# A hybrid decoder step on one core: where weight-block operations, gate stores and small stores stand in their queues

## The chip, the core and the metric

The kernel runs on one core of a Trainium2 chip. A core has five engines that each work through an instruction queue of their own, in order: TensorE (PE in the profile, its weight loads apart as PEld), VectorE (DVE), ScalarE (ACT), GpSimd (POOL) and SyncE (SP). Matrix products go from SBUF to PSUM by PE; DVE and ACT read PSUM and SBUF; GpSimd reads and writes SBUF alone. Transfers between the device's memory (DRAM below) and SBUF are issued as instructions of SP, ACT or POOL and carried out by 16 DMA engines that all three share. An instruction that waits for a semaphore holds everything behind it in its queue, a DMA issue as well as a computation.

The metric is the device time of one execution in microseconds. A time below is that of single executions, or the median over several.

## The reference

One decoder layer over a prompt of 2048 tokens and 8 single-token samples, all in f32, width 1024. Cut to what matters here:

```
hn  = rmsnorm(x) * (1 + scale) + shift              # shift, scale, gate from silu(c) @ w_ada + b_ada
xa, za, q, k, v, glr, zg = split(hn @ w_in)
xc  = conv4(xa); gx, ga = sigmoid(block-diagonal products of xc)
a   = exp(8 * ga * log_sigmoid(lambda))
h_t = a_t * h_(t-1) + sqrt(1 - a_t**2) * gx * xc    # the scan of the recurrence
y_lru = h * silu(za)
o, S = gated linear attention(q, k, v, log_sigmoid(glr @ w2 + b2) / 16)    # 4 heads, dk 128, dv 256
y_gla = rmsnorm(o) * silu(zg)
x   = x + gate * (concat(y_lru, y_gla) @ w_out);  y = rmsnorm(x)
```

## The kernel before

Every large product is made three times, as high*high, high*low and low*high parts in a fast number format, so each weight exists as a high and a low part. The prompt is worked in two halves of 1024 tokens. The main order is: for half 0, the four attention heads in the order 3, 0, 1, 2, each followed by one to three of the eight recurrence tiles; then a middle stage in which the gates `zg` and two recurrence tiles of half 1 are made by products over seven block combinations instead of eight (`seven`, `product`, L1511); then the four heads and five tiles of half 1; last the output projection (`Pair.product`, L1797), also with seven blocks. The ordinary projection is `project` (L650 to L652: 24 matmuls over 8 blocks of the width), the values are made by `value_mm` (L335 to L337: also 24).

The seven-block products need combinations of weight blocks. They are prepared on the side, during half 0 and half 1, by two chains of small steps:

- `pair_weights(n)`, n = 0 to 4, one pair of `w_in` column blocks each: two loads of 512 KB into the tile `tr` issued by POOL (L749), four DVE subtractions (L753) in two phases, then two phases in which ACT rounds (L758), DVE subtracts (L759) and POOL stores the parts to `twd` (L761). The tile has one buffer: the loads of pair n+1 wait until the stores of pair n have been read out. After the last phase the next pair's loads are issued.
- `out_weights`, steps s = 0 to 15, of `w_out`: two loads of 256 KB into `r` by POOL (L806), two DVE products with the gate `g` (L827), then four DVE subtractions (L827), for every second group of four steps two splits (ACT L831, DVE L832), and 7 to 9 stores to `wd` and `wd2` by POOL (L841, L834). Then the next step's loads are issued (`again`); at s = 0 and 8, and where the chain is taken up again, `begin` also loads the gate and waits longer.

Both run on a clock of their own, counted in units. `tick(u)` stands in the main program after each projection (1 unit for a projection of 264 to 512 columns, with exceptions of half a unit for each block of values and for `product`, and n/512 in `gates_ahead`), and `after(u, f)` puts f into a heap to be traced at the first tick that brings the clock to the present value plus u. So a delay in units is a delay in the order of the program, not in time. The phases inside a step follow at 0.5 units. `behind(V)` puts a step's DVE instructions directly behind the last DVE instruction traced before: whatever DVE instruction comes later in the program waits behind them.

`lru_last_a` sets `outw["stop"]` after the first of the last three recurrence tiles of half 0; the chain then ends with the step in hand, and `close_sp` takes it up again at the next step when half 1 begins.

The gates of half 0 are made in `gate_silu`; for the second part of the half it also makes the gate of the 8 samples, a tile of 128x8 (`zq`), and stores it (L1117). `xa_load` splits a recurrence tile's own small weights and stores the parts, 256 KB (L1331). `gates_seven` makes the gates of half 1 for three heads in the middle stage and stores each 128x512 tile to `zgd` from ACT (L1572); `gates_ahead` does so for the first head (L1599), each store right after its `silu2`. `silu` is an ACT instruction (L1092) and a DVE instruction (L1093); a store waits for the second.

## Time and profile before

| what | value |
|---|---|
| time, median of 3 executions | 1502.39 us (1500.59, 1502.39, 1505.2) |
| the profiled execution's own time | 1495.52 us |
| its span, from the first to the last instruction | 1493.7 us |
| mean granted TensorE clock in it | 0.989 of full |
| DMA, mean over the span | 204 GB/s; 9.6% of the DMA engines' time for what POOL issued, 46.4% SP, 4.3% ACT |

The profile is one execution. Its page gives each engine's busy time, then the same in 40 slices, the DMA queues, the chain of work that ended last, and the costliest groups of instructions. Further views list the waits (who waited for whom, how long in all, how often, the longest), all instructions in order of time (start, duration, engine, line, operation, tiles, shapes; in square brackets the idle time of the engine before it and what ended that), one line's instructions with their waits, and busy time, granted clock and DMA share in windows of time. "PE tp L1006 <- DVE xb L991" reads: PE, about to write the tile `tp` in line 1006, waited for DVE's write of `xb` in line 991. Idle time of an engine counts for the result only where PE, the busiest one, ends up waiting for it.

### The profile page before, as it was taken

To read this page: it belongs to the slowest core of one execution; us is meant where nothing else is said; L and a number is where in the kernel's file an instruction comes from. 1 tells how busy PE (TensorE), PEld (TensorE's weight loads), DVE (VectorE), ACT (ScalarE), POOL (GpSimd) and SP (SyncE) were. 2 spreads that over 40 slices of the span, in tenths; PEclk is the share of its full clock that TensorE was granted. 3 is DMA by queue.
4 is the path that set the end of the run, shared out by engine and by line. 5 is a ranking of instruction groups with operands and counts; after the bars stand their busy time and mean duration, and the time that the engine had idled before them with its cause. 6 is when DMAs were issued, how large, how long until landed. Compare 5 with 4: busy or idle time off the path is not lost.

```text
span 1493.7 us, 23572 instructions
## 1 busy us (share of the span) xinstructions
PE 1437.0 (96%) x8741; PEld 1259.8 (84%) x8741; DVE 1052.3 (70%) x2473; ACT 690.7 (46%) x1255; POOL 175.1 (12%) x288
## 2 busy tenths in 40 slices
PE   8999898999998999899999989999999999999998
PEld 6888877798887888777799989999998887778886
DVE  5757555766766678774539857576679887588886
ACT  4654443454355257634435453544556732244342
POOL 1200211222223121200011310000000000000000
PEclk9999999999999999999999999999999999999999
DMA  9656875667567466376865744635353757793452
GB/s 331 248 180 212 269 255 168 198 211 246 181 214 247 150 217 218 142 254 206 280 218 173 237 152 146 191 131 178 131 173 110 279 184 274 266 349 123 148 174 113
DMA packets 172120, 305.33 MB, mean 204 GB/s; under 512 B 13858, under 2 KB 103618, under 8 KB 169565
## 3 DMA queue, kind: packets, MB, share of 16 engines
q1 hardware_dynamic: 121333, 235.35, 46.4%
q0 software_dynamic: 16032, 48.28, 9.6%
q10 hardware_dynamic: 34640, 20.19, 4.3%
q8 instruction: 69, 1.13, 0.3%
q14 instruction: 46, 0.38, 0.1%
HBM read 188.51 MB, written 115.33 MB: 203 GB/s over the span
## 4 chain that ended last, share of the span: by engine, by line
PE 53%; DVE 5%; ACT 4%; DMA 3%; issue 2%; POOL 1%; ACTq 0%; POOLq 0%; DVEq 0%
PE acc L1797 12%; PE tp L1797 8%; PE acc L1511 6%; PE acc L650 5%; PE acc L652 5%; PE acc L651 5%; PE acc L335 1%; PE acc L337 1%; PE acc L336 1%; DMA w<-parts 1%; PE po L1040 1%; PE tp L1006 1%; DVE cv L1234 1%; ACT L945 1%; DMA wd<-r 1%
## 5 line engine op out<-in xcount | busy, mean ns | idle before, releaser
L650 PE MATMUL acc<-hh,w 128*128 128x512 f32 (+3 forms) x1112 | 388.5, 350 | 3.3 <-POOL hh L201 1.5
L651 PE MATMUL acc<-hl,w 128*128 128x512 f32 (+3 forms) x1112 | 377.0, 339 | 0.0
L652 PE MATMUL acc<-hh,w 128*128 128x512 f32 (+3 forms) x1112 | 376.7, 339 | 0.2 <-DVE w L300 0.2
L650 PEld LDWEIGHTS acc<-hh,w 128*128 128x128 f32 x1112 | 211.2, 190 | 23.2 <-POOL hh L201 2.4
L651 PEld LDWEIGHTS acc<-hl,w 128*128 128x128 f32 x1112 | 211.4, 190 | 16.5 <-DVE hl L202 0.2
L652 PEld LDWEIGHTS acc<-hh,w 128*128 128x128 f32 x1112 | 210.8, 190 | 17.0 <-DVE w L300 0.6
L1797 PE MATMUL acc<-w,a 128*128 128x512 f32 (+1 forms) x792 | 184.8, 386 | 0.0
L1797 PEld LDWEIGHTS acc<-w,a 128*128 128x128 f32 x792 | 146.8, 188 | 33.2 <-issue 3.4
L335 PE MATMUL acc<-w,hh 128*128 128x256 f32 (+1 forms) x508 | 146.4, 288 | 7.1 <-DVE vl L924 4.0
L337 PE MATMUL acc<-w,hl 128*128 128x256 f32 (+1 forms) x508 | 144.1, 284 | 0.2 <-DVE hl L225 0.2
L336 PE MATMUL acc<-w,hh 128*128 128x256 f32 (+1 forms) x508 | 143.8, 283 | 0.0
L1797 PE MATMUL tp<-w,a 128*128 128x512 f32 x564 | 136.0, 391 | 0.0
L1797 PEld LDWEIGHTS tp<-w,a 128*128 128x128 f32 x564 | 105.2, 188 | 26.8 <-issue 5.2
L335 PEld LDWEIGHTS acc<-w,hh 128*128 128x128 f32 x508 | 96.8, 191 | 10.1 <-DVE vl L924 4.6
L337 PEld LDWEIGHTS acc<-w,hl 128*128 128x128 f32 x508 | 97.1, 191 | 0.4 <-DVE hl L225 0.4
L336 PEld LDWEIGHTS acc<-w,hh 128*128 128x128 f32 x508 | 96.7, 190 | 0.1
L1234 DVE SCALAR_TENSOR_TENSOR cv<-xa,vecT,cv 128x512 f32<-128x512 f32 (+2 forms) x120 | 76.8, 644 | 9.1 <-ACT cv L1232 8.7
L1092 ACT ACTIVATE zs<-acc 128x512 f32<-128x512 f32 (+3 forms) x71 | 34.6, 489 | 102.6 <-PE acc L652 93.4
L1647 ACT CAST a<-s 128x512 fp32r<-128x512 f32 x61 | 36.5, 620 | 95.5 <-issue 36.2
L1093 DVE SCALAR_TENSOR_TENSOR zs<-zs,acc 128x512 f32<-128x512 f32 (+3 forms) x71 | 39.0, 549 | 45.5 <-ACT zs L1092 45.4
L923 ACT CAST vh<-acc 128x256 fp32r<-128x256 f32 x56 | 20.7, 371 | 78.9 <-PE acc L337 66.3
L924 DVE TENSOR_TENSOR vl<-acc,vh 128x256 fp32r<-128x256 f32 x56 | 23.4, 421 | 44.9 <-ACT vh L923 44.6
(389 smaller groups left out, 2713.3 us busy)
## 6 DMA issues: line engine op xcount, KB each, us to landing
parts<-w SPq DMA_DIRECT2D x37, 1024.0 KB
w<-parts SPq DMA_DIRECT2D x28, 1024.0 KB
wr<-in_w_in_dram SPq DMA_DIRECT2D x44, 512.0 KB
a<-mixd SPq DMA_DIRECT2D x63, 256.0 KB
w<-wd SPq DMA_DIRECT2D x12, 1024.0 KB
w<-twd SPq DMA_DIRECT2D x20, 512.0 KB
mixd<-zs ACTq DMA_DIRECT2D x34, 256.0 KB
wada<-in_w_ada_dram SPq DMA_DIRECT2D x16, 512.0 KB
```

What stands on the lines that cost most here:

```text
L335: PE.matmul(ps, hh[:, kt, c], hi[:, kt % 4], start=kt == 0, stop=False)
L336: PE.matmul(ps, hh[:, kt, c], lo[:, kt % 4], start=False, stop=False)
L337: PE.matmul(ps, hl[:, kt, c], hi[:, kt % 4], start=False, stop=kt == KT - 1)
L650: PE.matmul(ps[:, :n], hi[:, kt], a, start=kt == 0, stop=False)
L651: PE.matmul(ps[:, :n], hi[:, kt], b, start=False, stop=False)
L652: PE.matmul(ps[:, :n], lo[:, kt], a, start=False, stop=kt == KT - 1)
L1092: S.activation(z, ps, AF.Tanh, scale=0.5)
L1093: V.scalar_tensor_tensor(z, z, 1.0, ps, op0=OP.add, op1=OP.mult)
L1234: V.scalar_tensor_tensor(cv[:, cq], xa[:, cq.start + k:cq.stop + k], cw[k], cv[:, cq], op0=OP.mult, op1=OP.add)
L1511: PE.matmul(ps, w[:, u, k], x[v][k], start=start and (k, u, v) == (0, 0, 0), stop=(k, u) == (3, 1), skip_group_check=True)
L1647: S.copy(t[:, 0, k], (low(t) if src is None else src)[:, k])
L1797: PE.matmul(ps, t[:, u, k], w[:, v, k, c], start=(q < 3 or ps is own) and (k, u, v) == (0, 0, 0), stop=(k, u) == (3, 1), skip_group_check= ...
```

## The change

Six places, each a line:

```
 def pair_weights(n=0):
-        after(2, lambda: one([[sub(b11, b12, b11), ...
+        after(3, lambda: one([[sub(b11, b12, b11), ...
 def again(s, g):                                        # in out_weights
             r = load(s)
-            after(2, lambda: step(s, r, g))
+            after(3, lambda: step(s, r, g))
 def gate_silu(w, s, ct):
-                SP.dma_start(zgd[ct][:, TH:], q)
+                G.dma_start(zgd[ct][:, TH:], q)
 def xa_load(j, wx=True):
             parts[j] = dpool.tile([P, 2, 2, P], F32, tag=f"wg{j}", name="parts")
-            SP.dma_start(parts[j], wg.bitcast(F32))
+            G.dma_start(parts[j], wg.bitcast(F32))
 def gates_seven(n):
             silu(z, ps)
-            S.dma_start(zgd[2 * h + dt][:, s * 512:s * 512 + 512], z)
+            G.dma_start(zgd[2 * h + dt][:, s * 512:s * 512 + 512], z)
 def gates_ahead(h):
                 z = silu2(w[dt], c0, n)
-                S.dma_start(zgd[2 * h + dt][:, c0:c0 + n], z)
+                after(0.5, lambda z=z, dt=dt, c0=c0, n=n: S.dma_start(zgd[2 * h + dt][:, c0:c0 + n], z))
                 tick(n / 512)
```

In the two chains the first operations on a loaded block are traced three units after its loads instead of two. Eight stores of sample gates, eight of small weights and twelve of gates are issued by GpSimd (`G`) instead of SyncE or ScalarE. Six stores of gates stay on ScalarE and go through the heap with a delay of half a unit. What is computed is the same.

More of the change, by code (lines that the diff above doesn't have):

```diff
@@ L773, in pair_weights @@
         halves = [split(k, x) for k, x in enumerate((b11, b22, b12, b21))]
-        after(2, lambda: one([[sub(b11, b12, b11), sub(b12, b22, b12)], [sub(b22, b22, b11), sub(b21, b21, b22)],
+        after(3, lambda: one([[sub(b11, b12, b11), sub(b12, b22, b12)], [sub(b22, b22, b11), sub(b21, b21, b22)],
                                 halves[:2], halves[2:]]))
```

## The prediction

> **What bounds the kernel now.** I read the page's busy times first, then PE's idle gaps in order of time, then what DVE did in front of each, then the granted clock around them.

> ```profile
> span 1493.7 us, 23572 instructions
> PE 1437.0 (96%) x8741; PEld 1259.8 (84%) x8741; DVE 1052.3 (70%) x2473; ACT 690.7 (46%) x1255; POOL 175.1 (12%) x288
> ```

> PE is the bound: busy for 1437.0 of 1493.7 us. The 56.7 us in which it sits idle are all that a change of order can win directly. These are its longest gaps after the start:

> ```profile
> 170.33 0.58 PE L335 MATMUL acc<-w,hh 128*128 128x256 f32 x1 [3.98 <-DVE vl L924]
> 197.46 0.38 PE L1006 MATMUL tp<-xb,e 128*128 128x128 f32 x1 [2.48 <-DVE xb L991]
> 238.63 1.94 PE L1126 MATMUL tp<-ident,on 128*128 128x128 f32 x8 [6.38 <-DVE on L1053]
> 279.59 0.59 PE L1271 MATMUL acc<-xh,wg 128*128 128x264 f32 x1 [3.51 <-DVE zs L1093]
> 480.17 0.58 PE L1006 MATMUL tp<-xb,e 128*128 128x128 f32 x1 [4.11 <-DVE xb L991]
> 875.52 0.73 PE L1006 MATMUL tp<-xb,e 128*128 128x128 f32 x3 [3.45 <-DVE xb L991]
> ```

> Each waits for DVE, for a different line each time, so the named lines aren't the cause. What is common to them stands a few microseconds earlier in DVE's queue:

> ```profile
> 168.23 0.69 DVE L753 TENSOR_TENSOR tr<-tr 128x512 f32<-128x512 f32 x1 [5.87 <-DMA tr<-in_w_in_dram]
> 195.39 1.42 DVE L753 TENSOR_TENSOR tr<-tr 128x512 f32<-128x512 f32 x2 [2.28 <-DMA tr<-in_w_in_dram]
> 231.55 0.69 DVE L753 TENSOR_TENSOR tr<-tr 128x512 f32<-128x512 f32 x1 [6.17 <-DMA tr<-in_w_in_dram]
> 278.25 0.69 DVE L753 TENSOR_TENSOR tr<-tr 128x512 f32<-128x512 f32 x1 [6.58 <-issue]
> 464.45 1.29 DVE L827 TENSOR_TENSOR r<-r,g 128x512 f32<-128x512 f32 x2 [4.84 <-DMA r<-in_w_out_dram]
> 465.78 0.41 ACT L831 CAST p<-r 128x256 fp32r<-128x256 f32 x1 [6.75 <-DVE r L827]
> 866.86 0.69 DVE L827 TENSOR_TENSOR r<-r,g 128x512 f32<-128x512 f32 x1 [4.23 <-DMA r<-in_w_out_dram]
>   DMA r<-in_w_out_dram: 17.6, 6
> ```

> DVE reaches the first operation on a weight block before the block has landed, and everything of the main path queued behind it (value evictions, normalisation, decay) waits too; at 464 ACT is held as well, by the split behind the same load. (The row at 278.25 names "issue"; its operation is the same, the first on a pair.) The last row is from the view of line 827: its 32 products waited for loads 17.6 us in 6 waits; two of them, over 3 us each, reached no PE gap of this size.

> A gap costs more than its idle time. The windows view, cut where the granted clock changes:

> ```profile
> 169.30:176.10 6.80, 5.77 (x28) 0.50 0.58 211
> 237.60:244.40 6.80, 5.77 (x25) 0.50 0.34 103
> 278.50:285.30 6.80, 5.71 (x26) 0.50 0.47 154
> 479.90:483.30 3.40, 3.13 (x13) 0.50 1.01 323
> 875.90:879.30 3.40, 3.40 (x15) 0.51 0.32 107
> ```

> Columns: window, length, PE busy (matmuls), granted clock, DMA share and GB/s. Around every gap of 3.45 us or more PE ran at half clock, 3.4 or 6.8 us long; around the one of 2.48 us it didn't. The busy time in them is 5.77 + 5.77 + 5.71 + 3.13 + 3.40 = 23.8 us; half of it, **11.9 us**, is lost. [...]

> **The change part by part: the third unit.** It removes no work. It moves the first DVE operation on a block one unit later in program order. What it must beat is the time from the last store of the block before to the landing of the new one. For a pair:

> ```profile
> 149.09 1.08 POOL L761 DMA_DIRECT2D twd<-tr  x2 [0.92 <-DVE tr L759]
> 154.27 0.92 POOL L749 DMA_DIRECT2D tr<-in_w_in_dram  x1 [4.10 <-DMA twd<-tr]
> 160.80 0.90 POOL L749 DMA_DIRECT2D tr<-in_w_in_dram  x1 [5.61 <-issue]
> DMA to landing us min/median/max: 4.5/6.4/8.7
> ```

> From the last store's issue (149.6) the two loads are issued at 154.3 and 160.8, and DVE starts on the data at 168.2: 18.6 us. How long a unit is follows from the matmul spacing:

> ```profile
> 165.97 0.28 PE L336 MATMUL acc<-w,hh 128*128 128x256 f32 x1
> 166.08 0.28 PE L337 MATMUL acc<-w,hl 128*128 128x256 f32 x1
> 286.14 0.40 PE L651 MATMUL acc<-hl,w 128*128 128x512 f32 x1
> 286.38 0.40 PE L652 MATMUL acc<-hh,w 128*128 128x512 f32 x1
> ```

> Starts are 0.11 us apart at 256 columns, 0.24 at 512. So 24 matmuls take 2.7 us for a block of values (half a unit), 2.8 for a 256- or 264-column projection and 5.6 for 512 columns (a unit each); 384 columns, between them, 4.2. Counting ticks through the loops I find which projections lie between load and first operation:

> - Pair 1 now: one of 264 columns and two blocks of values, 8.2 us; after: six blocks, 16.2. That is 8.0 more for a stall of 5.87.
> - Pair 2: three blocks and a 512 (13.7), then three of 512 (16.8): 3.1 more for 2.28.
> - Pair 3: two of 512 (11.2), then 256 + 264, 512 and 256 (14.0): 2.8 more for 6.17, short by 3.4. The chunk products of the attention head, also between them, shrink that.
> - Pair 4: 256 + 264 (5.6), then 264 + 512 + 512 (14.0): 8.4 more for 6.58.
> - `w_out` step 7, the stall at 464: four blocks (10.8), then three of 512 (16.8): 6.0 more for 4.84.
> - Step 15, the stall at 867: four blocks (10.8), then three of 384 (12.6): 1.8 more for 4.23, short by 2.4.

> What is taken from each PE gap is the smaller of gap and stall, for 480 the gap, since ACT's longer wait hung on that load too: 3.98 + 2.28 + 6.17 + 3.51 + 4.11 + 3.45 = **23.5 us**, and 11.9 of clock with it: 35.4. What stays, where the added time falls short: 3.4 + 2.4 = 5.8 at most, 0 at least with the chunk products. I take **3.0**. Both are below the gaps at which the clock fell.

> The steps also shift. The five pairs end at unit 36.5 instead of 32, and the `w_out` chain has done 8 steps instead of 12 when it is stopped, so that four more (steps 8 to 11, each six DVE operations and nine POOL transfers) run in half 1, up to unit 142.5 of 165.5, where before it was done at 123.5. They fit. What they cost there:

> ```profile
> 752.00:885.00 133.00, 126.75 (x942) 122.69 (x941) 91.92 (x302) 61.03 (x126) 30.77 (x53) 0.99 0.59 196
> 885.00:1010.00 125.00, 123.82 (x928) 118.80 (x926) 85.64 (x306) 57.77 (x126) 4.94 (x8) 1.00 0.46 148
> ```

> With four steps (752 to 885) PE idled 6.25 us, 3.45 of them the gap counted above; without steps 1.18. So four more steps cost 6.25 - 3.45 - 1.18 = **1.6 us**; the bounds are 0 and 2.8. DVE, 69% busy in both windows, has room.

> **The stores.** Sample gates and small weights leave SP's queue for POOL's, 0.55 us an issue. What they held up on SP:

> ```profile
> SPq L1117 <- DVE zq L1093: 80.1, 7, 24.7
> SPq L1331 <- DVE wg L1329: 37.8, 5, 15.4
> PE acc L652 <- DVE w L300: 0.2, 1, 0.2
> ```

> SP waited 117.9 us on these, with weight loads behind it, yet the one PE wait in half 0 for a freshly loaded weight is the 0.2 in the last row. The cover is the loads issued ahead; the gain is at most 0.2. On POOL each wait now stands in front of the block loads and stores traced after it. Those follow DVE instructions placed later still, so the wait is hidden as long as POOL keeps program order; if not, it is the slower rival below. Taken as 0.

> The twelve gates of the middle stage leave ACT for POOL, which does next to nothing there. Gain: at most PE's wait for ACT in that stage, 0.7 us; loss: a gate buffer that comes free later, bounded by the only wait of that kind (2.5 us, ACT for an earlier store). Taken as 0.

> ```profile
> PE acc L1511 <- ACT acc L1525: 0.7, 1, 0.7
>   ACT zs L1092: 2.5, 1
> 613.57 0.56 ACT L199 ACTIVATE ra<-tp,Sh,Gm 128x256 f32<-128x256 f32 x1 [4.99 <-DVE zs L1093]
> ```

> The half unit in `gates_ahead` mostly does nothing: the store goes into the heap and the very next line ticks by 0.5 or 1, which takes it out again. So ACT's 4.99 us before 613.57, spent at the first of these stores, stays. Only the fourth, due at unit 82 with the last gates of recurrence tile 7, falls behind those. That may gain or lose about a microsecond of ACT's time; 0.

> **Sum**, against the profiled execution's own 1495.5: -23.5 - 11.9 + 3.0 + 1.6 = -30.8, thus 1464.7. That execution lies 6.9 us below the median of the three shown, 1502.4; from the median it would be 1471.6. One stall more or less is worth some 6.5 us (3.5 idle, 2.9 of clock), so I hold part of that difference for stalls that also go. I take **1469 us**.

> **Rivals.**

> *The unit is too short where it counts.* Loads that land later than in this one execution, up to 8.7 us after issue where 6.4 is the median, bring back pairs 3 and 4 and step 15 in part. For: two places fall short by my count. Against: pairs 1, 4 and step 7 have 1 us or more to spare. If a third of 35.4 stays, the time is 1469 + 12 = 1481.

> *The wait only moves.* The blocks' transfers are late because the DMA engines are, and the main path's DVE work lies wherever the step falls; as many PE gaps appear elsewhere. For: DMA share 0.47 to 1.01 in the windows above. Against: of 32 products on `w_out` blocks 26 waited for no load. Time 1500, no change.

> *POOL's queue becomes the bound (slower).* In half 0 the sample stores hold POOL as they held SP, 80.1 / 7 = 11.4 us each, with the next block's loads behind them. This decides once the hold is longer than the 5.6 us of the added unit: then DVE stalls by 5.8 us again, which at 170 cost 3.98 + 2.9 = 6.9 us. Seven times that is 48: 1469 + 48 = 1517. Against it stands the order on POOL, as above, and how evenly its issues run:

> ```profile
> L761 POOL DMA_DIRECT2D twd<-tr x20: 542/542/552, 145.1 to 291.6; - x20
> ```

> [...]

> **How the numbers follow.** Forecast 0.73, unit too short 0.13, wait moves 0.05, POOL 0.09. A difference of 0.3% (4.5 us) is about what a measurement of this kernel can tell from no change. The first two are faster, the third the same, the fourth slower: 0.86, 0.05, 0.09. The forecast's own range is 1457 to 1481: from the profiled execution with nothing staying and another 3 us from the stores, to the median with 5.8 and 2.8 staying and some 5 lost at the stores. The range that also holds the second case and its worse half reaches to 1494.

> **What would show it.** Right: no DVE idle of over 2 us in front of L753 and L827; PE's idle down from 56.7 to about 38; no half clock between 20 and 1480 us; L827 from about 350 to 1000 us with its last 16 products, not 8, after 750. The store steps: L1117, L1331 and L1572 on POOL, SP's waits on the first two gone and replaced by waits for buffers, the 4.99 of ACT still there. Wrong: DVE waiting for `tr` or `r` as before (the unit), gaps of 3.4 us and more with other releasers (the wait moved), or POOL idle at L1117 and L1331 just ahead of late L749 or L806 loads.

## The result and the profile after

The changed kernel took 1477.72 us (median of 4 executions, 1475.09 to 1479.32), the kernel before, on the same chip, 1501.49 us (4 executions, 1492.67 to 1505.2). The ratio is 0.985 with a 95% interval of 0.980 to 0.989: faster by 23.8 us, where 1469 us had been forecast. The profiled execution of the changed kernel took 1479.32 us, the longest of its four, that of before was 6 us below its median; the two traces therefore differ by 16.2 us only, and the split below is of those 16.2.

From the page of the changed kernel, its first lines:

```profile
span 1477.5 us, 23587 instructions
PE 1434.1 (97%) x8741; PEld 1258.6 (85%) x8741; DVE 1050.0 (71%) x2472; ACT 690.6 (47%) x1255; POOL 188.1 (13%) x314
```

PE's idle time fell from 56.7 to 43.4 us, 13.3 less; its busy time from 1437.0 to 1434.1 us, 2.9 less. Forecast were 18.9 less idle (-23.5 + 3.0 + 1.6) and 11.9 less of half clock.

Busy time by stage, before first, then the changed kernel (columns as before: window, length, PE busy and matmuls, PEld, DVE, ACT, POOL, granted clock, DMA share, GB/s; the stages begin up to 30 us earlier in the changed kernel, the windows are the same):

```profile
100.00:300.00 200.00, 183.56 (x1168) 163.81 (x1167) 126.99 (x301) 83.11 (x158) 32.00 (x52) 0.95 0.64 209
300.00:560.00 260.00, 255.52 (x1476) 225.34 (x1475) 180.70 (x397) 124.37 (x206) 63.62 (x109) 0.99 0.64 209
560.00:760.00 200.00, 191.81 (x1018) 159.79 (x1017) 130.88 (x219) 99.48 (x152) 21.06 (x31) 1.00 0.66 225
760.00:1140.00 380.00, 367.83 (x2730) 352.82 (x2729) 266.62 (x877) 188.55 (x393) 38.48 (x66) 1.00 0.51 168
```

```profile
100.00:300.00 200.00, 197.19 (x1309) 176.20 (x1308) 138.42 (x317) 96.80 (x176) 32.42 (x54) 1.00 0.68 226
300.00:560.00 260.00, 260.00 (x1460) 227.48 (x1460) 178.62 (x397) 129.37 (x213) 52.06 (x90) 1.00 0.60 201
560.00:760.00 200.00, 190.20 (x1050) 162.97 (x1049) 117.83 (x210) 89.62 (x141) 23.27 (x36) 0.97 0.62 209
760.00:1140.00 380.00, 362.21 (x2673) 347.23 (x2672) 283.70 (x901) 190.53 (x395) 59.36 (x102) 0.99 0.53 173
```

Length less PE busy is PE's idle time. Before 560 us it falls from 16.4 + 4.5 to 2.8 + 0.0, by 18.1. From 560 to 760 it grows from 8.2 to 9.8, and from 760 to 1140 from 12.2 to 17.8. The first half pays most of what was forecast for it (18.1 of 20.1); the rest gives 7.2 us of it back.

PE's rows in order of time, at its long gaps:

```profile
177.29 0.51 PE L650 MATMUL acc<-hh,w 128*128 128x512 f32 x1 [0.91 <-DVE vl L924]
613.44 0.57 PE L1511 MATMUL acc<-hh,w 128*128 128x512 f32 x1 [3.74 <-DVE zs L1093]
724.13 0.60 PE L335 MATMUL acc<-w,hh 128*128 128x272 f32 x1 [3.38 <-DMA w<-parts]
844.49 0.41 PE L650 MATMUL acc<-hh,w 128*128 128x384 f32 x1 [2.18 <-DMA w<-parts]
941.22 0.49 PE L650 MATMUL acc<-hh,w 128*128 128x384 f32 x1 [5.05 <-DVE xb L973]
1120.39 0.44 PE L1271 MATMUL acc<-xh,wg 128*128 128x384 f32 x1 [2.64 <-ACT tx L1274]
```

All six gaps that the prediction listed are gone; the first row is what is left of the one at 170. The others are where no gap of 3 us stood before, and the half clock came with them. (The last one is not new: before, PE waited 2.4 us for the same write, at full clock.) The windows view, cut where the granted clock changes:

```profile
613.70:617.10 3.40, 3.40 (x9) 2.68 (x9) 3.40 (x4) 2.03 (x4) 0.00 (x0) 0.51 1.04 332
723.00:729.80 6.80, 5.67 (x25) 5.67 (x26) 0.71 (x4) 0.37 (x1) 2.11 (x3) 0.50 1.04 308
845.80:849.20 3.40, 3.40 (x12) 3.40 (x11) 0.47 (x1) 0.00 (x0) 1.65 (x3) 0.51 0.42 148
941.40:944.80 3.40, 3.40 (x12) 3.40 (x12) 0.56 (x2) 0.82 (x2) 1.44 (x2) 0.50 0.96 371
1122.30:1125.70 3.40, 3.40 (x17) 3.33 (x16) 3.32 (x5) 2.73 (x6) 0.00 (x0) 0.50 0.00 0
```

PE was busy for 19.3 us in these, so 9.6 us are lost to the clock where 11.9 were lost before.

DVE's waits, from the order of time and from the views of lines 753 and 827:

```profile
175.16 0.69 DVE L753 TENSOR_TENSOR tr<-tr 128x512 f32<-128x512 f32 x1 [5.00 <-DMA tr<-in_w_in_dram]
209.64 0.69 DVE L753 TENSOR_TENSOR tr<-tr 128x512 f32<-128x512 f32 x1 [4.41 <-DMA tr<-in_w_in_dram]
930.62 0.69 DVE L827 TENSOR_TENSOR r<-r,g 128x512 f32<-128x512 f32 x1 [3.37 <-DMA r<-in_w_out_dram]
...
  DMA tr<-in_w_in_dram: 9.4, 2
...
  DMA r<-in_w_out_dram: 3.4, 1
```

Two of the pairs (1 and 2) still stall DVE, by 5.0 and 4.4 us, where it was 5.87 and 2.28. PE pays nearly nothing for these. The windows view over the first two of DVE's waits, and below it over the wait of before that ended at 168.23:

```profile
170.16:175.16 5.00, 5.00 (x46) 4.94 (x42) 0.00 (x1) 0.00 (x0) 0.00 (x0) 1.00 1.06 374
205.23:209.64 4.41, 4.41 (x21) 3.60 (x21) 0.00 (x1) 0.36 (x1) 0.00 (x0) 1.00 0.82 252
```

```profile
162.36:168.23 5.87, 3.99 (x36) 3.80 (x34) 0.00 (x1) 0.00 (x0) 0.00 (x0) 1.00 1.00 271
```

Before, PE had 3.99 us of work for a wait of 5.87 and ran dry while DVE still waited; now it is busy through the whole wait. The stall of pair 1 is nearly as long as it was and stands where PE has more work ahead.

The stores are where the change puts them (a line's view: issues, ns, first and last):

```profile
L1117 POOL DMA_DIRECT2D zgd<-zq x8: 541/546/570, 111.1 to 497.9; - x8
...
L1572 POOL DMA_DIRECT2D zgd<-zq x8: 542/542/543, 667.4 to 719.2; - x8
```

### The profile page after: what moved, and what is told of

It reads as the page before. It is cut to its first block, busy times and chain, and to the rows that moved or that the text cites. A ratio compares the mean times of both kernels' runs of the same rounds, so it can differ in the third digit from the quotient of the medians.

```text
span 1477.5 us, 23587 instructions
## 1 busy us (share of the span) xinstructions
PE 1434.1 (97%) x8741; PEld 1258.6 (85%) x8741; DVE 1050.0 (71%) x2472; ACT 690.6 (47%) x1255; POOL 188.1 (13%) x314
## 4 chain that ended last, share of the span: by engine, by line
PE 65%; DVE 9%; DMA 6%; ACT 5%; issue 3%; POOL 0%; ACTq 0%; DVEq 0%; SPq 0%; POOLq 0%
PE acc L1797 12%; PE tp L1797 9%; PE acc L650 8%; PE acc L652 8%; PE acc L651 8%; PE acc L1511 6%; PE acc L335 2%; PE acc L337 2%; PE acc L336 2%; DMA w<-parts 1%; DMA mixd<-zs 1%; PE po L1040 1%; DMA xt<-in_state_gla_dram 1%; PE tp L1006 1%; PE acc L1271 1%
## 5 line engine op out<-in xcount | busy, mean ns | idle before, releaser
L651 PE MATMUL acc<-hl,w 128*128 128x512 f32 (+3 forms) x1112 | 377.4, 339 | 0.0
L652 PE MATMUL acc<-hh,w 128*128 128x512 f32 (+3 forms) x1112 | 377.0, 339 | 0.0
L651 PEld LDWEIGHTS acc<-hl,w 128*128 128x128 f32 x1112 | 210.9, 190 | 16.6 <-DVE hl L202 0.4
L652 PEld LDWEIGHTS acc<-hh,w 128*128 128x128 f32 x1112 | 210.8, 190 | 16.5
L335 PE MATMUL acc<-w,hh 128*128 128x256 f32 (+1 forms) x508 | 146.0, 287 | 5.4 <-DMA w<-parts 3.4
L337 PE MATMUL acc<-w,hl 128*128 128x256 f32 (+1 forms) x508 | 143.7, 283 | 0.0
L336 PE MATMUL acc<-w,hh 128*128 128x256 f32 (+1 forms) x508 | 143.6, 283 | 0.0
L335 PEld LDWEIGHTS acc<-w,hh 128*128 128x128 f32 x508 | 96.8, 191 | 7.9 <-DMA w<-parts 3.6
L337 PEld LDWEIGHTS acc<-w,hl 128*128 128x128 f32 x508 | 97.1, 191 | 0.0
L336 PEld LDWEIGHTS acc<-w,hh 128*128 128x128 f32 x508 | 96.7, 190 | 0.1
L1647 ACT CAST a<-s 128x512 fp32r<-128x512 f32 x61 | 36.5, 620 | 95.8 <-issue 36.8
L1092 ACT ACTIVATE zs<-acc 128x512 f32<-128x512 f32 (+3 forms) x71 | 34.6, 488 | 93.8 <-PE acc L652 84.7
L1093 DVE SCALAR_TENSOR_TENSOR zs<-zs,acc 128x512 f32<-128x512 f32 (+3 forms) x71 | 38.9, 548 | 41.7 <-ACT zs L1092 41.7
L165 ACT ACTIVATE junk<-on 128x256 bf16<-128x256 f32 x64 | 26.6, 416 | 71.7 <-DVE on L1045 70.3
```

What stands on the lines that cost most here:

```text
L335: PE.matmul(ps, hh[:, kt, c], hi[:, kt % 4], start=kt == 0, stop=False)
L336: PE.matmul(ps, hh[:, kt, c], lo[:, kt % 4], start=False, stop=False)
L337: PE.matmul(ps, hl[:, kt, c], hi[:, kt % 4], start=False, stop=kt == KT - 1)
L651: PE.matmul(ps[:, :n], hi[:, kt], b, start=False, stop=False)
L652: PE.matmul(ps[:, :n], lo[:, kt], a, start=False, stop=kt == KT - 1)
L1092: S.activation(z, ps, AF.Tanh, scale=0.5)
```

## The experiments

Each kernel differs from one of the two by the lines shown. "Before" is the kernel before, measured beside it on the same chip: 1500.33 us for the first four runs, 1501.85 for the next four, 1501.03 for the three with one and four units, 1497.62 for the last.

**The delays alone, and the stores alone.** The first keeps the two delays of three units and undoes all four edits of stores; the second is its complement (delays back to 2).

```
-                G.dma_start(zgd[ct][:, TH:], q)                # the three other stores, too, as they were before
+                SP.dma_start(zgd[ct][:, TH:], q)
```

> Only the two delays are three units; all stores are where they were before. Theory A (the added unit carries the gain, the stores are worth nothing): ratio to before 0.984, within 0.980 to 0.988, none of the six long PE gaps of before, and the gap of about 5 us at step 14 still there. Theory B (the stores carry part of it): ratio 0.990 or more. Theory C (the stores cost what is missing from the forecast, 7 us): ratio 0.980 or less, without the PE gaps near 613 and 724.

> The delays are two units again, the four store edits stay. Theory A: ratio 0.998 to 1.002, and DVE waits for tr and r as in before, 38 us in all. Theory B: 0.995 or less. Theory C (stores on GpSimd hold the block loads): 1.004 or more, with longer DVE waits for tr and r than before's.

Delays alone: 1475.51 us, ratio 0.984 (0.9815 to 0.9866). Stores alone: 1504.45 us, ratio 1.0028 (1.0007 to 1.005). The delays bring the whole gain, some 25 us, as theory A had it (six gaps gone, the one at step 14 there). The stores cost 4 us (1 to 8) without the delays; beside them it is 2 us (1477.72 against 1475.51), which these executions do not resolve. Rows of PE, delays alone:

```profile
936.39 0.66 PE L650 MATMUL acc<-hh,w 128*128 128x384 f32 x1 [5.27 <-DVE S L1020]
```

Stores alone:

```profile
640.96 0.80 PE L1511 MATMUL acc<-hh,w 128*128 128x512 f32 x1 [3.73 <-DVE zs L1093]
752.93 0.59 PE L335 MATMUL acc<-w,hh 128*128 128x272 f32 x1 [3.66 <-DMA w<-parts]
```

The gap near 940 belongs to the delays. (In two of the traces below, with `gates_seven` back and without the half unit, it is put down to a weight load, `w<-parts`, 5.75 and 4.70 us; with DVE's wait gone, in the run with four units for the last steps, PE waits no longer than 1.2 us there.) The two at 613 and 724 of the changed kernel stand in the second kernel too, some 28 us later because its first half is slower. DVE's waits at L753 and L827 were 34.4 us with the stores moved and 38.5 before; POOL's queue held no block load back long enough to show. So the time lies between theories A and C, and C's cause, held block loads, is not what costs it.

**Which store makes which gap.** Three kernels undo one part of the changed kernel's stores each: the twelve gates of `gates_seven` back on ACT, the half unit in `gates_ahead` away, the small stores back on SP.

```
-            G.dma_start(zgd[2 * h + dt][:, s * 512:s * 512 + 512], z)
+            S.dma_start(zgd[2 * h + dt][:, s * 512:s * 512 + 512], z)
```

```
-                after(0.5, lambda z=z, dt=dt, c0=c0, n=n: S.dma_start(zgd[2 * h + dt][:, c0:c0 + n], z))
+                S.dma_start(zgd[2 * h + dt][:, c0:c0 + n], z)
```

```
-                G.dma_start(zgd[ct][:, TH:], q)
+                SP.dma_start(zgd[ct][:, TH:], q)
...
-            G.dma_start(parts[j], wg.bitcast(F32))
+            SP.dma_start(parts[j], wg.bitcast(F32))
```

> As the changed kernel, but the twelve gate stores of the middle stage are issued by ScalarE again. If those stores, landing together with the value weights of half 1, make the PE gap of 3.4 us near 724 (and its 6.8 us at half clock), the gap falls below 2 us and the time lies 3 to 6 us under the changed kernel's, ratio 0.981. Rival (the weights land that late anyway and PE merely gets there earlier): the gap stays between 2 and 4 us and the ratio is 0.984 to 0.986.

> As the changed kernel, but the stores of the first head's gates are traced at once again. If the fourth of them, now behind the last gates of recurrence tile 7, holds ACT or a gate buffer and makes the PE gap of 3.7 us near 613, that gap falls below 1.5 us and the ratio is about 0.981. Rival (the half unit does nothing, the gap comes from the two 512-column gates waiting for buffers that the recurrence's outputs hold): the gap stays at 3 to 4 us and the ratio is 0.984 to 0.986.

> The changed kernel with the two small stores (sample gates zq, small weights wg) back on SP's queue. Theory (they are hidden on either queue; the extra PE gaps near 613 and 724 us come from the two edits of the gates' stores): time as the changed kernel, 1477 +- 4; SP waits on L1117 and L1331 again, about 80 and 38 us, and no PE gap follows from it; the gaps of 3.4 to 4 us near 613 and 724 stay; DVE's waits at L753 stay near 9 us in 2. Rival (on POOL these stores hold back the block loads queued behind them): L753's waits fall to under 4 us and the time to 1471.

| kernel | gates_seven on | half unit | gap near 613 | wait for `w<-parts` near 724 | time, ratio (95%) |
|---|---|---|---|---|---|
| changed | POOL | yes | 3.74 | 3.38 | 1477.72, 0.985 (0.980 to 0.989) |
| gates_seven back | ACT | yes | 3.71 | 0.28 | 1480.14, 0.988 (0.985 to 0.991) |
| half unit away | POOL | no | 1.57 | 3.97 | 1477.53, 0.986 (0.984 to 0.989) |
| small stores back | POOL | yes | 3.77 | 3.44 | 1481.18, 0.986 (0.983 to 0.988) |
| delays alone | ACT | no | 1.88 | 1.25 | 1475.51, 0.984 (0.982 to 0.987) |

The two gaps follow the two edits of the gates' stores, each its own, in every kernel; the small stores make neither. (What stays near 613 without the half unit, 1.57 and 1.88 us, waits for a weight load.) The times don't resolve them: each is worth 2 to 3 us of idle time and at most 3 of clock, and the executions of one kernel spread over 4 to 9 us. The gain of 3 to 6 us that was expected of `gates_seven` on ACT, and the ratio of 0.981 expected of both, did not come (0.988 and 0.986). With the small stores back DVE's waits at L753 stay too (8.5 us in 2), as its theory had it, so on POOL these stores don't hold the block loads back.

How the half unit does it is in ACT's rows, changed kernel first, then the one without the half unit:

```profile
607.45 0.60 ACT L1092 ACTIVATE zs<-acc 128x512 f32<-128x512 f32 x1 [0.73 <-PE acc L652]
609.95 1.00 ACTq L664 DMA_DIRECT2D mixd<-zs  x2
610.99 1.04 ACT L1448 CAST so<-fs 128x1024 fp32r<-128x1024 f32 x1 [2.94 <-DVE zs L1308]
611.94 0.59 ACT L1092 ACTIVATE zs<-acc 128x512 f32<-128x512 f32 x1
```

```profile
608.34 0.60 ACT L1092 ACTIVATE zs<-acc 128x512 f32<-128x512 f32 x1 [0.48 <-PE acc L652]
609.47 0.60 ACT L1092 ACTIVATE zs<-acc 128x512 f32<-128x512 f32 x1 [0.53 <-PE acc L652]
612.96 0.98 ACTq L664 DMA_DIRECT2D mixd<-zs  x2
```

L1092 is the gates' activation, on whose accumulator PE's next product waits. Without the half unit ACT does two of them in a row. With it, the stores of the recurrence tile (L664) come between them in ACT's queue; they wait for DVE's output of the recurrence (L1308), ACT stands for 2.94 us, and the second activation starts at 611.94 instead of 609.47.

The other gap, in POOL's rows of the changed kernel, and in ACT's and POOL's rows with `gates_seven` back on ACT:

```profile
716.40 0.54 POOL L1572 DMA_DIRECT2D zgd<-zq  x1 [3.97 <-DVE zq L1093]
719.23 0.54 POOL L1572 DMA_DIRECT2D zgd<-zq  x1 [2.29 <-DVE zq L1093]
719.83 0.73 POOL L786 DMA_DIRECT2D g<-gated  x1
724.13 0.73 POOL L806 DMA_DIRECT2D r<-in_w_out_dram  x1 [0.48 <-issue]
```

```profile
718.46 0.33 ACTq L1572 DMA_DIRECT2D zgd<-zq  x1
...
720.91 0.62 ACTq L1572 DMA_DIRECT2D zgd<-zq  x1
...
700.83 0.78 POOL L786 DMA_DIRECT2D g<-gated  x1 [98.83 <-PE acc L1511]
```

SP issues the value weights that PE waits for at the same time in both (711.8). On POOL the last gate stores leave about 2 us earlier, and the load of `g`, held behind them in POOL's queue, 19 us later: both fall into the time in which the value weights land, with the DMA engines' share at 1.0 in both kernels. That the store's place makes the gap is shown; which of these transfers delays the weights is not.

**Pairs alone, steps alone.** From the kernel before, one delay each:

```
-        after(2, lambda: one([[sub(b11, b12, b11), ...
+        after(3, lambda: one([[sub(b11, b12, b11), ...
```

```
-            after(2, lambda: step(s, r, g))
+            after(3, lambda: step(s, r, g))
```

> The kernel before with the third unit for the pairs alone; steps on w_out blocks two units behind, stores as before. The four gaps of before at 170, 197, 239 and 280 us are 15.9 us of idle and, with three windows of 6.8 us at half clock, 8.7 us of clock: 24.6. Theory A (the gaps' prices hold): 1500 - 24.6 + 1.5 = 1477, waits at L753 about 9 us in 2, gaps of over 3 us left only behind L827. Theory B (prices are too high throughout; the units alone gained 24.8 of 35.4, so each term by 0.7): 1483. Rival (the gain comes from the steps, not the pairs): 1490 or more.

> The kernel before with the third unit for the w_out steps alone; pairs two units behind, stores as before. The two gaps at 480 and 876 us are 7.6 us of idle and, with two windows of 3.4 us, 3.3 us of clock: 10.8. Theory A: 1500 - 10.8 = 1489 if no step meets a new stall, 1494 if one like that near 936 us in the run with both units comes (5.3 us idle at half clock). The four gaps between 170 and 281 us stay at 3 to 6 us with half clock. Theory B (by 0.7): 1492. Rival (gain from the steps): 1480 or less.

Pairs alone: 1476.04 us, ratio 0.9825 (0.980 to 0.985). Steps alone: 1492.59 us, 0.994 (0.991 to 0.996). Both are as the gaps' prices had it (1477, and 1489 to 1494). But they don't add: 26 and 9 us alone, 25 together. With the pairs alone the stall of before at 464, and the PE gap of 4.11 behind it, is gone although the steps still run two units after their loads: none of the 18 products before 750 us waits. With the steps alone it is gone too, so both single runs have this gain. The pairs now end later, and the whole chain of steps falls on other places of the main path. Its new bad place is in the second half; DVE, pairs alone:

```profile
836.84 0.69 DVE L827 TENSOR_TENSOR r<-r,g 128x512 f32<-128x512 f32 x1 [9.09 <-DMA r<-in_w_out_dram]
```

**One unit.** The kernel before with both delays at 1.

> The kernel before with one unit, not two, between a block's load and its first operation, for pairs and steps; stores as before. Theory (the stall is the landing time less the units, so it grows by the unit taken away, 2.8 to 5.6 us): DVE waits at L753 rise from 20.9 us in 4 to some 35 us in 5, at L827 from 17.6 us in 6 to over 50 us in 12 or more; each stall past 3 us costs PE its idle time and a window of half clock, so some 12 more of them at 4 to 5 us: 1545 to 1570. Rival (late loads come from busy DMA engines and not from the distance in the program): waits within a third of before's, time under 1512.

1517.67 us, ratio 1.011 (1.007 to 1.014). DVE's waits, views of lines 753 and 827:

```profile
  DMA tr<-in_w_in_dram: 37.1, 4
...
  DMA r<-in_w_out_dram: 38.9, 14
```

The waits double, from 38.5 to 76.0 us, as the first theory has it, though those at L827 stay below what it expected (35 us at L753, over 50 at L827); a rival in which the program's distance does not matter is out. The time does not follow: 1545 to 1570 was expected, and PE's idle time grows from 56.7 to 77.2 us only. Behind two waits of 14.3 and 16.0 us at the pairs PE idled 16.1 and 13.6 us; in the stretch of the 14 waits at L827 it has three gaps of over 3 us. A stall of DVE has no fixed price.

**Four units for the last steps.** The kernel with the delays alone, and

```
-            after(3, lambda: step(s, r, g))
+            after(3 + s // 8, lambda: step(s, r, g))
```

> Both delays three units and all stores as before (the kernel that took 1475.5), and beside it a fourth unit for the steps of the second half (8 to 15). There step 14's load landed 8.0 us after its issue, DVE waited 3.3 us and PE idled 5.3 us near 936 us at half clock. Theory (the wait is the load's, and another unit covers it): no DVE wait of over 1 us at L827 after 750 us, no gap of over 3 us and no half clock between 25 us and the end; 1475.5 - 5.3 - 1.7 = 1468.5. Rival (it moves to another step, or comes from the six blocks of values there): a gap of 3 to 5 us at another place, 1474 to 1477.

1475.41 us, ratio 0.982 (0.980 to 0.985). L827 waits for no load any more and the gap near 936 is gone, as the theory has it; the time of 1468.5 was missed, and the rival's, 1474 to 1477 with a gap at another place, held. In the trace another of the same kind has come, at the first operation on a block of the last stage:

```profile
1001.88 0.69 DVE L1916 TENSOR_TENSOR wr<-wr 128x512 f32<-128x512 f32 x1 [3.50 <-DMA wr<-mixd]
...
1004.26 0.58 PE L335 MATMUL acc<-w,hh 128*128 128x256 f32 x1 [3.79 <-ACT vs L893]
```

**The last stage's blocks three units behind.** On top of it, `after(2 + 0.75 * k, f)` became `after(3 + 0.75 * k, f)` for the list that L1916 begins.

> The same kernel of 1475.4, and beside it the first operations on the last stage's early blocks (the list that begins with L1916) three units after their loads, not two. There DVE waited 3.50 us at L1916 for a load that landed 8.3 us after its issue, and PE idled 3.79 us behind it near 1004 us with 3.4 us of half clock. Theory (the same kind of wait, with the same cure): that wait and that gap go, no half clock between 30 and 1100 us, 1475.4 - 3.8 - 1.7 = 1470. Rival (the wait moves on to the next of the list, or the splits come too late for the last stage's first products): a gap of 3 us or more between 1000 and 1130 us, 1475 or more.

1475.62 us, ratio 0.983 (0.980 to 0.986), the wait at L1916 3.26 us and the PE gap 3.55. The edit did not move L1916: the instructions ahead of it in DVE's queue are the same in both kernels, and only later ones of the list moved. So the run says nothing about that wait.

**Four units for the pairs.** Once on top of the kernel with four units for the last steps, once with three for all steps.

```
-        after(3, lambda: one([[sub(b11, b12, b11), ...
+        after(4, lambda: one([[sub(b11, b12, b11), ...
```

> The kernel with three units, a fourth for steps 8 to 15 and stores as before (1475.4), and a fourth unit for the pairs too. There DVE still waits 3.7 and 4.7 us at L753, near 175 and 210 us. Theory (PE has work for these, so they cost nothing): both waits gone, time within 4 us of 1475; one step fewer in the first half, one more in the second. Rival (they still cost the time that the gaps of before cost): 1475 - 8 = 1467.

> Four units for the pairs, three for all steps, stores as before: one number away from the kernel of 1468.6 (there steps 8 to 15 have four) and one from the kernel of 1475.5 (there the pairs have three). Theory (the pairs' two DVE waits of 3.7 to 5 us, left at three units, do cost time in most executions, although hardly in the profiled ones): 1470 or less, no wait at L753. Rival (it was the steps' place and their fourth unit): 1474 to 1478, with a DVE wait of over 2 us at L827 after 750 us and a PE gap of over 4 us behind it.

With both at four: 1468.57 us (6 executions, 1467.94 to 1472.42), ratio 0.978 (0.976 to 0.981). With four for the pairs alone: 1476.21 us, 0.986 (0.983 to 0.989). No wait at L753 is left in either. In the second, six waits at L827 came (11.5 us), in the first three (3.0 us). Of the expectations for the first kernel the rival's time held (1467, where the theory had 1475 within 4); of those for the second the rival's time and DVE waits did, but not its PE gap of over 4 us (the longest is 3.28 us). So the fastest of these kernels has both delays at four and the stores as they were; its slowest execution is below the fastest of the changed kernel. Why both are needed isn't settled: neither fourth unit alone gave a gain that these runs resolve, and the profiled execution of the kernel with both, 1471.4 us, is among its longest, while that of the kernel with three for the pairs, 1471.4 us too, is its shortest. The 7 us between their medians lie in executions without a trace. Of these the mean granted clock is known: 0.994 or more in five of six executions of the kernel with both, in two of six of the one with three for the pairs and in two of six of the one with three for the steps; the lowest is 0.990. So part of the 7 us goes with time at half clock; what brings that on in some executions only stays open.

## Why the prediction was right, and where it was off

*Direction and mechanism.* Right. PE bounds the kernel, and the gain came from first operations on blocks that had not landed: moved one unit, all six listed gaps went, and the delays alone give 0.984. The rivals "wait only moves" (no change) and "POOL's queue becomes the bound" (slower) are out; the time lies nearer to the 1481 of "unit too short" than to 1469, but not for that reason: pairs 3 and 4 and step 15, which it named, did not stall. The range held the time, 1457 to 1494.

*The idle term of 23.5.* Right for the first five gaps: 20.1 of it lie before 560 us, and 18.1 were won there. The sum's reason was wrong for two. Pair 1 was to have 8.0 us more for a stall of 5.87, and pair 2 enough too; DVE still waited 5.00 and 4.41 us there. That these two gaps went all the same was the luck of the place, not of the count. The failed step is the length of a unit, taken from the spacing of PE's matmuls. In the changed kernel, POOL's row of the last store of pair 0 and DVE's rows just ahead of its wait:

```profile
156.83 0.54 POOL L761 DMA_DIRECT2D twd<-tr  x1 [0.82 <-DVE tr L759]
...
167.02 0.42 DVE L924 TENSOR_TENSOR vl<-acc,vh 128x256 fp32r<-128x256 f32 x1 [2.30 <-ACT vh L923]
169.74 0.42 DVE L924 TENSOR_TENSOR vl<-acc,vh 128x256 fp32r<-128x256 f32 x1 [2.29 <-ACT vh L923]
```

From the store's end to the begin of the wait 12.8 us passed (157.4 to 170.2), where 12.2 had passed before (150.2 to 162.4): the unit gave 0.6 us, not 8.0. The blocks of values between are those that the prediction counted, two before and six now. But before, DVE did not keep PE's pace: it was busy for 9.4 of its 12.2 us, with the recurrence tile's operations, so that the stretch counted as 8.2 us took longer anyway. In the changed kernel it was busy for 7.9 of 12.8 us, and at the end it waited for the values, one block every 2.7 us, which is PE's pace. At the place to which the unit moved the wait, PE had work for all of it.

*The clock term of 11.9.* Mis-sized most: about 2.3 (11.9 lost before, 9.6 after). Every window was to go, and five others came. In the trace of the delays alone only one stretch of half clock is left between 100 and 1450 us, 3.4 us long with 2.9 us of PE's work: there the term came nearly whole. Of the five in the changed kernel, those at 613 and 723 follow the stores' gaps; the one near 845 follows a gap that the delays alone have too (1.83 us idle from 836.9 to 840.3, at full clock), the one near 1122 a wait that took 2.40 us before, at full clock. Half of the busy time is also a little too much: from 941.5 to 944.7 us of the changed kernel, at a granted clock of 0.50, products of 384 columns start 0.32 us apart, and 0.17 to 0.18 us from 944.9 on, which is 0.45 us lost for each us busy at half clock.

*Residual 3.0 and extra steps 1.6.* The two places named as short, pair 3 and step 15, did not stall; step 14 did, by 3.37 us, and PE idled 5.05 us behind it. The prediction compared the added time only at places that had stalled before; the chain, once shifted, met new ones in every version whose last steps run two or three units behind. With the eight steps now in it, the stage from 760 to 1140 idles 5.6 us more instead of 1.9 less (1.6 - 3.45). Not all of that is step 14: with four units for the last steps, where L827 waits for no load, the stage still idles 16.2 us, against 12.2 before and 17.8 in the changed kernel; and 3.79 of its 16.2 lie behind the new wait at L1916.

*The stall at 464 counted for the steps' unit.* The steps' unit removes it, but the pairs' unit alone does so too, by moving the chain. The prediction's terms were each put down to one of the two delays, and this one belongs to either.

*The stores at nothing.* Mis-sized by about 4 us (2 beside the delays, not resolved). Small stores: right, as far as the times tell. That the half unit "mostly does nothing" and the fourth store "may gain or lose about a microsecond" was wrong: ACT's gap of 4.99 before became one of 3.50 at the same work, but PE got a new one of 3.74. `gates_seven` on POOL was bounded by waits for ACT and for a buffer; what it cost was a wait for weights in flight (3.38 us against 0.28), which had no term at all. That the stores' own transfers and the shifted load of `g` delay these weights is likely by the rows above, and not shown.

*The median.* 7 us were between the profiled execution and the median, and part of this was kept for stalls that the trace of before did not show. The delays alone won 22.5 us between traces (1493.7 to 1471.2) and 24.8 between medians, where the forecast had 30.8. The granted clock bears out the reason: 0.989 in the profiled execution of before, 0.986 in the median of the 50 executions of that kernel beside the runs above, the longer ones having mostly the lower clock.

## What to carry to other kernels

Price a stall of a side chain by what PE has queued at that moment, not by its own length: a wait of 5.0 us cost PE 0.9 in one place, one of 5.9 cost 4.0 in another. When a chain is delayed, list where all of its later steps land, not only the steps that stalled. A store is not free because nobody waits for it: its place in its issuer's queue is part of the move (half a unit's delay of six stores made a PE gap of 3.74 us where 1.57 stands without it), and so, likely, is the moment at which it meets a load on the DMA engines (a wait of 3.38 us for weights where 0.28 stands with these stores on ACT).

## What the runs showed of the hardware

```profile
566.00:569.40 3.40, 1.66 (x10) 1.11 (x9) 3.40 (x10) 2.41 (x5) 0.63 (x1) 1.00 0.51 102
842.40:845.80 3.40, 1.31 (x8) 1.34 (x9) 3.04 (x11) 1.41 (x4) 0.00 (x0) 1.00 1.02 393
1118.90:1122.30 3.40, 1.76 (x9) 1.41 (x9) 3.40 (x7) 2.99 (x7) 0.00 (x0) 1.00 0.00 0
```

After the second and third, with PE idle for 2.1 and 1.6 us, the clock fell for one window; after the first, idle for 1.7, it did not. In these two traces all ten falls from full clock follow a window on the grid with 1.64 us or more of PE's idle time, and no window with more than 1.89 us (before, 230.7 to 234.1) is followed by full clock; between the two either happened. The gap of 2.48 us before, split over two windows (1.6 and 0.9 us), cost no clock, and one of 2.18 us at 844 did.
